# Attention by hand-ordered matmuls: inverse roots by log and exp, other buffers for the compression weights, memory heads further apart, half of the convolution taps held back

## The chip, the cores and the metric

The kernel runs on one core of a Trainium2 chip. The metric is the device time of one execution in microseconds (us); the median of three runs is compared. The engines are called as the profile calls them: PE (matrix products; PEld its weight loads), DVE (vector), ACT (scalar and activation), POOL (general), SP (whose queue issues the DMAs).

## The reference

Two transformer blocks are applied to 256 tokens of width 1024, in float32. Block one mixes stick-breaking attention and gated linear attention (GLA), then a squared-ReLU MLP. Block two is a hybrid layer:

```
q_nsa, kv_nsa, g_nsa, conv_in, q_mem, g_merge = split(rms_norm(x) @ w_in)
kc = rms_norm(compress(k_c)); vc = compress(v_c)     # compress: gelu(blocks @ w1) @ w2
o_nsa = g[0]*attend(q, kc, vc) + g[1]*attend(q, ks, vs) + g[2]*attend(q, kw, vw)   # 8 heads, g = sigmoid(g_nsa)
u = silu(layer_norm(depthwise_conv31(a * sigmoid(ag)) + conv_b))   # 512 channels
o_m = softmax(qm @ km.T) @ vm                        # 4 memory heads of 128, 256 memory tokens
merged = gm[0]*(o_nsa @ w_nsa_out) + gm[1]*(u @ w_conv_out) + gm[2]*(o_m @ w_mem_out)   # gm = sigmoid(g_merge)
h = x + merged @ w_out;  out = h + (silu(hn @ w_gate) * (hn @ w_up)) @ w_down
```

## The kernel before, in words

**The stream of weights.** Every float32 operand of a large product is split into a high and a low part. A chunk of weights (128 x 1024, 512 KB) is brought by SP into one of four buffers `raw`, ACT casts it to `hi` (L519, three buffers), DVE subtracts to get `lo` (L523, three buffers), and PE adds hi times hi, hi times low and lo times high (L325, L327, L329: eight matmuls each for a column tile with eight row blocks). So each chunk needs SP, ACT, DVE and PE in this order, and a `hi` buffer is free when PE has finished with it. Buffers are taken in turn: a chunk that is late holds up the one three places behind it.

**Who sets the order.** A scheduler lists the instructions by priority (`tc.high_priority` raises it, `tc.issue_after` forbids an instruction before another one) and fixes for each engine one order. On the chip each engine works through its order strictly, so an instruction that waits holds up all behind it. In block two's attention the order on PE is written by hand (`manual_schedule`): `fill(gates, n)` puts n halves of a merge gate's column tile (`gm`, one chunk each) between the steps of the attention, as work that needs nothing of the attention. DVE, ACT and SP are ordered by the scheduler there too.

**Block two's attention, by its functions.** `compress` multiplies the keys and values by the compression weights `wc1` (L1213) and ends with a gelu that is written with a sigmoid (`cmp_t`, `cmp_h`) and a norm of the compressed keys (`cmp_k`, `cmp_kn`, L1256 to L1260). `nsa_operands` sums squares by head (L1276), takes an inverse root by integer shift and three Newton steps (`rsqrt`, twelve small DVE instructions, L385 to L391, into `hn_y`) and transposes it (L1291). `nsa` runs eight score blocks `first(n)`, transposes (`turned`, L1393), products (`values`, L1407) and the compressed branch (L1329). `mem_attention` is a generator with three parts for each of four memory heads: scores (L1461) and softmax; transposes of the probabilities P (L1476); product with the values (L1482), whose result is split into `om`. `conv_taps` adds 31 shifted products for each of four channel groups on DVE (L1494, L1496), and `conv_norm` makes the layer norm from them: a mean over channels by a matmul (L1511), a subtraction, squares, token sums (L400), an inverse root of two columns (twelve DVE instructions), its transpose back (L407), a product, a sigmoid and the split `uc`. Behind the attention stand three products with the branches' output weights: `wmo` (operand `om`), `wno` (operand `on`), `wco` (operand `uc`).

**Block one.** In GLA, `gla_scores` takes a gate's decay by a cumulative sum, six pairs of scaled operands `lev` (L779 to L783, two of the products on POOL or DVE), and masks sums `lvm` (L813, L816).

Of the kernel before, what the change touches and what calls it, by code (L numbers as in the profile page):

```python
# [183 lines left out]
class Kern:  # L184
# [65 lines left out]
    def load_constants(self):  # L250
# [123 lines left out]
    def rsqrt(self, v, n, y=None):  # L374

        nc = self.nc
        if n > 16:
            ti, hv, t = self.small("rw_i", [128, n], I32, bufs=1), *(self.small(s, [128, n], bufs=1) for s in ("rw_h", "rw_t"))
        else:
            ti = self.gsmall("rs_i", [128, 16], I32)[:, :n]  # L380
            hv = self.gsmall("rs_h", [128, 16])[:, :n]
            t = self.gsmall("rs_t", [128, 16])[:, :n]
# [41 lines left out]
    def split(self, h, l, src, gain=None):  # L424
# [4 lines left out]
        if gain is None:  # L429
            nc.scalar.copy(h, src)  # L430
            nc.vector.tensor_tensor(l, src, h.bitcast(F32), op=OP.subtract)
        else:
            nc.scalar.activation(h, src, AF.Copy, scale=gain)
            nc.vector.scalar_tensor_tensor(l, src, gain, h.bitcast(F32), op0=OP.mult, op1=OP.subtract)

# [122 lines left out]
def block_one(K, B, after):  # L558
# [4 lines left out]
    st = K.stream("w1a")  # L563
    for q in range(4):
# [12 lines left out]
    for k in range(8):  # L577
        xk = xin[k // 4][:, (k % 4) * 256:(k % 4) * 256 + 256]
        K.split(X.h(k), X.l(k), xk, par["norm_mix"][:, k:k + 1])
    for q in range(4):  # L580
        sqs.add(xin[q // 2][:, (q % 2) * 512:(q % 2) * 512 + 512])
    rc, rr = None, None
# [22 lines left out]
    def norm():  # L605
        nonlocal rc, rr
# [105 lines left out]
def gla_scores(K, glow, wgu, gq, gk):  # L712
# [22 lines left out]
    K.tap("c", c)  # L735

# [36 lines left out]
    def level(w):  # L773
# [8 lines left out]
        nc.gpsimd.tensor_tensor(gv[:, :, 1], ev[:, :, 1], qv[:, :, 1], op=OP.mult)  # L782
# [14 lines left out]
    for pr in range(3):  # L797
# [17 lines left out]
        if pr:  # L815
            nc.gpsimd.tensor_tensor(m, m, sums, op=OP.add)  # L816
# [9 lines left out]
def gla_values(K, SS, gv, og):  # L826
# [4 lines left out]
    for h in range(4):  # L831
# [9 lines left out]
        nc.gpsimd.tensor_tensor(s[:, :256], s[:, :256], s[:, 256:], op=OP.add)  # L841
# [189 lines left out]
def block_two(K, B, KM, vm, out):  # L1031
# [54 lines left out]
    with tc.manual_schedule(engines={mybir.EngineType.PE}):  # L1086
# [7 lines left out]
        nc.vector.tensor_tensor(gn, K.gemm_n(K.narrow("wgn", B.gain), B.x), rr, op=OP.mult)  # L1094
# [9 lines left out]
        s4 = nc.scalar.activation(N.gate, pg, AF.Sigmoid)  # L1104
# [6 lines left out]
        with tc.issue_after(s3.ins), tc.issue_after(s4.ins), tc.issue_after(N.sig.ins):  # L1111
# [3 lines left out]
    conv_taps(K, u, cv)  # L1115
# [70 lines left out]
def compress(K, kc2, N):  # L1186
# [381 lines left out]
```

## Time and profile before

| what | value |
|---|---|
| median of three runs | 945.62 us (944.42 to 948.03) |
| the profiled execution's own time | 948.07 us |
| its span | 946.3 us |
| PE busy | 907.4 us (96%) |
| DVE busy | 675.7 us (71%) |
| ACT busy | 495.6 us (52%) |
| POOL busy | 69.7 us (7%) |
| mean granted TensorE clock | 0.982 |

The span runs from the first to the last instruction; the time of the run holds 1.8 us more. The profiled execution took 2.45 us longer than the median. PE has work for nearly the whole span, so what can be taken away is mainly its idle time and the time in which its clock is granted at half. The clock has two levels, 1.2 and 2.4 GHz; a granted clock of 0.50 in a row is the lower one.

### The profile page before, as it was taken

Reading aid. Unit: us, or ns where it says so; the run is one execution under the profiler, and the core shown is the slowest. Engines: PE = TensorE matmul, PEld = TensorE weight load, DVE = VectorE, ACT = ScalarE, POOL = GpSimd, SP = SyncE. Lnnn points to the kernel's source line nnn. Section 1 sums busy time; section 2 is a strip of 40 time slices with the busy share of each in tenths; the row PEclk is TensorE's granted clock in tenths of the full one; section 3 lists DMA queues with packets and bytes.
Section 4 is the critical chain, followed back from the end, with each engine's and each line's share of the span. In section 5 each row is a group of like instructions: output and inputs, shape, how many; then the busy total and the mean of one; then the engine's idle time right before and its main releaser. Section 6 shows DMA issues by size and latency. Waiting matters only on the chain.

```text
span 946.3 us, 17011 instructions
## 1 busy us (share of the span) xinstructions
PE 907.4 (96%) x6816; PEld 834.7 (88%) x6816; DVE 675.7 (71%) x1167; ACT 495.6 (52%) x745; POOL 69.7 (7%) x94
## 2 busy tenths in 40 slices
PE   8988999999999999999999886988899999999998
PEld 6986789999999999888999786977799988888887
DVE  6698758857776665556568958897488878888653
ACT  5555665644555554444443245666854655555432
POOL 1022012200010000011200000000003200000000
PEclk9999999999999999999999979899999999999999
DMA  7644325665756566566655743222346556666672
GB/s 268 200 128 128 102 70 155 217 201 178 223 179 183 184 189 181 157 184 192 185 174 167 266 124 112 68 89 90 112 117 191 184 176 181 187 191 182 192 208 65
DMA packets 44287, 155.64 MB, mean 164 GB/s; under 512 B 5040, under 2 KB 6576, under 8 KB 44208
## 3 DMA queue, kind: packets, MB, share of 16 engines
q1 hardware_dynamic: 43776, 153.48, 52.4%
q8 instruction: 53, 0.87, 0.4%
q10 hardware_dynamic: 432, 1.08, 0.4%
q14 instruction: 26, 0.21, 0.1%
HBM read 153.49 MB, written 1.05 MB: 163 GB/s over the span
## 4 chain that ended last, share of the span: by engine, by line
PE 85%; DVE 6%; ACT 4%; DMA 2%; issue 2%; POOL 1%; SPq 0%; DVEq 0%; ACTq 0%; POOLq 0%
PE pj L296 17%; PE pj L325 15%; PE pj L327 14%; PE pj L329 14%; PE pj L297 9%; PE pj L368 5%; DVE lo L523 2%; ACT hi L519 2%; PE pj L310 1%; PE pj L311 1%; PE pj L309 1%; DVE cv L1496 1%; DMA raw<-in_w2a_dram 1%; POOL lev L782 1%; PE pt L1276 1%
## 5 line engine op out<-in xcount | busy, mean ns | idle before, releaser
L519 ACT CAST hi<-raw 128x1024 fp32r<-128x1024 f32 x276 | 288.3, 1047 | 302.3 <-PE pj L327 125.7
L523 DVE TENSOR_TENSOR lo<-raw,hi 128x1024 fp32r<-128x1024 f32 x276 | 343.0, 1244 | 116.7 <-ACT hi L519 110.7
L296 PE MATMUL pj<-hid,hi 128*128 128x512 f32 x378 | 134.3, 400 | 0.0
L296 PE MATMUL pj<-xf,hi 128*128 128x512 f32 x320 | 113.2, 399 | 0.0
L297 PE MATMUL pj<-hid,lo 128*128 128x256 f32 x378 | 106.2, 281 | 0.0
L297 PE MATMUL pj<-xf,lo 128*128 128x256 f32 x320 | 89.8, 281 | 0.0
L296 PEld LDWEIGHTS pj<-hid,hi 128*128 128x128 f32 x378 | 71.0, 188 | 17.5
L296 PEld LDWEIGHTS pj<-xf,hi 128*128 128x128 f32 x320 | 60.1, 188 | 14.8
L297 PEld LDWEIGHTS pj<-hid,lo 128*128 128x128 f32 x378 | 71.4, 189 | 0.0
L297 PEld LDWEIGHTS pj<-xf,lo 128*128 128x128 f32 x320 | 60.4, 189 | 0.0
L325 PE MATMUL pj<-xm,hi 128*128 128x256 f32 x336 | 55.1, 310 | 0.0
L325 PEld LDWEIGHTS pj<-xm,hi 128*128 128x128 f32 x336 | 48.5, 209 | 4.2 <-issue 2.7
L1496 DVE SCALAR_TENSOR_TENSOR cv<-u,par,cv 128x256 f32<-128x256 f32 x120 | 51.5, 477 | 0.0
L472 POOL TENSOR_TENSOR acc<-acc,ffr 128x256 f32<-128x256 f32 (+1 forms) x25 | 27.3, 1099 | 311.4 <-ACT ffr L465 288.9
L327 PE MATMUL pj<-xm,hi 128*128 128x256 f32 x336 | 49.7, 293 | 0.0
L329 PE MATMUL pj<-xm,lo 128*128 128x256 f32 x336 | 47.9, 286 | 0.0
L327 PEld LDWEIGHTS pj<-xm,hi 128*128 128x128 f32 x336 | 46.2, 204 | 0.0
L327 PE MATMUL pj<-xn,hi 128*128 128x256 f32 x304 | 44.2, 285 | 0.0
L329 PEld LDWEIGHTS pj<-xm,lo 128*128 128x128 f32 x336 | 44.2, 195 | 0.0
L329 PE MATMUL pj<-xn,lo 128*128 128x256 f32 x304 | 43.9, 284 | 0.0
L325 PE MATMUL pj<-xn,hi 128*128 128x256 f32 x304 | 43.5, 285 | 0.0
L329 PEld LDWEIGHTS pj<-xn,lo 128*128 128x128 f32 x304 | 39.5, 192 | 0.5 <-issue 0.4
(464 smaller groups left out, 1653.3 us busy)
## 6 DMA issues: line engine op xcount, KB each, us to landing
raw<-in_wf_dram SPq DMA_DIRECT2D x64, 512.0 KB, 3.7
raw<-in_wgu_dram SPq DMA_DIRECT2D x44, 512.0 KB, 3.7
raw<-in_w1g_dram SPq DMA_DIRECT2D x24, 512.0 KB, 3.7
raw<-in_w2g_dram SPq DMA_DIRECT2D x24, 512.0 KB, 3.7
raw<-in_wdn_dram SPq DMA_DIRECT2D x22, 512.0 KB, 3.7
raw<-in_w2a_dram SPq DMA_DIRECT2D x20, 512.0 KB, 3.7
raw<-in_w1a_dram SPq DMA_DIRECT2D x16, 512.0 KB, 4.7
raw<-in_wo_dram SPq DMA_DIRECT2D x16, 512.0 KB, 3.7
```

The costliest lines, as they stand in the source:

```text
L296: mm(ps, lhsT=st.hi(w), rhs=x.both(k), start=k == 0, stop=False, skip_group_check=True)
L297: mm(ps[:, :T], lhsT=st.lo(w), rhs=x.h(k), start=False, stop=k == kt - 1, skip_group_check=True)
L309: mm(ps[:, j], lhsT=st.hi(w), rhs=x.h(k), start=k + j == 0, stop=False, skip_group_check=True)
L310: mm(ps[:, j], lhsT=st.hi(w), rhs=x.l(k), start=False, stop=False, skip_group_check=True)
L325: mm(ps[:, j], lhsT=st.hi(o + k), rhs=x.h(k), start=k == 0, stop=False)
L327: mm(ps[:, j], lhsT=st.hi(o + k), rhs=x.l(k), start=False, stop=False)
L329: mm(ps[:, j], lhsT=st.lo(o + k), rhs=x.h(k), start=False, stop=k == kt - 1)
L368: mm(pss[t], lhsT=xx(k)[:, t * 128:t * 128 + 128], rhs=ww(o + k), start=k == 0 and xx == x.h and ww == st.hi, stop=k == kt - 1 and ww == s ...
L472: self.engine.tensor_tensor(a, a, s, op=OP.add)
L519: nc.scalar.copy(hi, raw)
L523: eng.tensor_tensor(lo[:, o:o + n], raw[:, o:o + n], hi[:, o:o + n].bitcast(F32), op=OP.subtract)
L1496: nc.vector.scalar_tensor_tensor(o, u[:, c, k:k + 256], w[:, c, k:k + 1], o, op0=OP.mult, op1=OP.add)
```

## The change

It has five groups of edits.

- **Start.** A fourth warm-up matmul; the first two chunks of `w1a` are brought, cast and subtracted in halves (`st.halved`); the splits of the input get priorities and the squares stand behind the last of them.
- **Block one.** The decay of GLA is computed in a function of its own (`gla_decay`) and called in the norm's lead; twelve instructions go from POOL to DVE: six `lev` products, two `lvm` sums and four sums `ffr`.
- **Compression weights.** They are brought as 16 DMAs of 128 x 512 into the four buffers `P1` of the attention's probabilities instead of 8 of 128 x 1024 into `raw`.
- **Sigmoid and inverse root.** Both sigmoids (gates and gelu) become max, Exp, plus one, reciprocal; the inverse roots of `hn_y` and of `cmp_k` become Ln, Exp and three DVE instructions (one Newton step).
- **Memory heads and taps.** The parts of a memory head stand further apart among the `fill(gates, 1)`; the taps of channel groups 2 and 3 may be issued only behind the softmax denominators of score blocks 4 and 7 (`N.marks`).

```diff
@@ start
-            for _ in range(3):
-                nc.tensor.matmul(p, lhsT=z[:, :128], rhs=z, start=True, stop=True)
+            for n in (512, 512, 512, 256):
+                nc.tensor.matmul(p[:, :n], lhsT=z[:, :128], rhs=z[:, :n], start=True, stop=True)
...
+    st.halved = (0, 1)
...
+        with tc.high_priority(offset=800000 - 50000 * k):
+            last = K.split(X.h(k), X.l(k), xk, par["norm_mix"][:, k:k + 1])
+    with tc.issue_after(last.ins):
+        for q in range(4):
+            sqs.add(xin[q // 2][:, (q % 2) * 512:(q % 2) * 512 + 512])
@@ block one
             nc.vector.tensor_tensor(glow, ps, rr, op=OP.mult)
+            decay = gla_decay(K, glow, wgu)
...
-        nc.gpsimd.tensor_tensor(gv[:, :, 1], ev[:, :, 1], qv[:, :, 1], op=OP.mult)
+        nc.vector.tensor_tensor(gv[:, :, 1], ev[:, :, 1], qv[:, :, 1], op=OP.mult)
...
-            nc.gpsimd.tensor_tensor(m, m, sums, op=OP.add)
+            nc.vector.tensor_tensor(m, m, sums, op=OP.add)
...
-        nc.gpsimd.tensor_tensor(s[:, :256], s[:, :256], s[:, 256:], op=OP.add)
+        nc.vector.tensor_tensor(s[:, :256], s[:, :256], s[:, 256:], op=OP.add)
@@ compress
-            with K.tc.high_priority(offset=100000):
-                raw = K.wp.tile([128, 1024], F32, tag="raw", name=K.nm("wc1"), bufs=4)
-                nc.sync.dma_start(raw, K.a["wc1"][kv * 4 + ch])
             for j in range(4 * ch, 4 * ch + 4):
-                w = raw[:, (j % 4) * 256:(j % 4) * 256 + 256]
+                if j % 2 == 0:
+                    raw = K.small("P1", [128, 2, 256], bufs=4)
+                    with K.tc.high_priority(offset=100000):
+                        nc.sync.dma_start(raw, K.a["wc1"][kv * 4 + ch][:, (j % 4) * 256:(j % 4) * 256 + 512])
...
-    N.sig = nc.scalar.activation(t, t, AF.Sigmoid, scale=2 * (2 / np.pi) ** 0.5)
+    sigmoid(K, t, t, 2 * (2 / np.pi) ** 0.5)
...
-    y = K.rsqrt(k2, 16)
+    y = rsqrt_exp(K, k2, *(K.small(n, [128, 16], bufs=1) for n in ("cmp_y", "cmp_w")))
+def sigmoid(K, out, x, scale=1.0):
+    K.nc.vector.tensor_scalar(out, x, -87.0 / scale, None, op0=OP.max)
+    K.nc.scalar.activation(out, out, AF.Exp, scale=-scale)
+    K.nc.vector.tensor_scalar(out, out, 1.0, None, op0=OP.add)
+    K.nc.vector.reciprocal(out, out)
+def rsqrt_exp(K, v, y, t):
+    nc.scalar.activation(t, v, AF.Ln)
+    nc.scalar.activation(y, t, AF.Exp, scale=-0.5)
+    nc.vector.tensor_tensor(t, y, y, op=OP.mult)
+    nc.vector.scalar_tensor_tensor(t, t, -0.5, v, op0=OP.mult, op1=OP.mult)
+    nc.vector.scalar_tensor_tensor(y, t, 1.5, y, op0=OP.add, op1=OP.mult)
@@ nsa
+        N.marks[n] = nc.vector.tensor_tensor(den, den, gate[:, :, 3 * h + 1:3 * h + 3], op=OP.mult)
...
         values(i)
-        if m:
-            finish(m)
         fill(gates, 1)
+        if i:
+            next(late[-1 - (i == 3)])
         if i < 3:
-            m = mem(i)
-            next(m)
+            late.append(mem(i))
+            next(late[-1])
+        fill(gates, 1)
+        if i:
+            finish(late[-2])
+        if i < 2:
             fill(gates, 1)
@@ block_two, conv_taps
-    conv_taps(K, u, cv)
+    conv_taps(K, u, cv, {2: N.marks[4], 3: N.marks[7]})
...
+        with K.tc.issue_after(behind[c].ins) if c in behind else nullcontext():
```

The edits shift the lines: in the changed kernel L325, L327, L329 are L324, L326, L328; L523 is L522; L1461, L1476, L1482 are L1497, L1512, L1518; L1496 is L1534; L1511, L400, L407 are L1549, L396, L403.

**PE, memory head 0.** Ahead of the change these rows stand on PE (con is the identity that a transpose multiplies by; pj is a column tile's sum, hi and lo are named by their chunk):

```order
L1461 MATMUL pt_6668<-km_2500,qm_5252 128x256 x2
L325 MATMUL pj_6637<-xm_4405,hi_6683 128x256 x2
...
L329 MATMUL pj_6637<-xm_4408,lo_6684 128x256 x2
L1393 MATMUL pt_6712<-con,P_950_6499 128x128
...
L1476 MATMUL pt_6724<-con,P_982_6675 128x128 x4
```

And with the change:

```order
L1497 MATMUL pt_6680<-km_2507,qm_5259 128x256 x2
L324 MATMUL pj_6649<-xm_4412,hi_6695 128x256 x2
...
L324 MATMUL pj_6724<-xm_4412,hi_6727 128x256 x2
...
L324 MATMUL pj_6724<-xm_4412,hi_6796 128x256 x2
...
L324 MATMUL pj_6837<-xm_4412,hi_6840 128x256 x2
...
L324 MATMUL pj_6837<-xm_4412,hi_6909 128x256 x2
...
L1512 MATMUL pt_6938<-con,P_986_6687 128x128 x4
```

Between the scores of the head and the transposes of its probabilities stood one chunk of gates; now five stand there, with attention steps among them.

**PE, the convolution's norm.** Before, the token sums and the transposed inverse root stood in these rows:

```order
L400 MATMUL pt_7584<-con,ffr_7574 128x1 x2
L329 MATMUL pj_7382<-xm_4405,lo_7421 128x256 x2
...
L325 MATMUL pj_7649<-om_5235,hi_7652 128x256 x2
...
L329 MATMUL pj_7649<-om_5236,lo_7653 128x256 x2
L325 MATMUL pj_7713<-om_5235,hi_7716 128x256
L407 MATMUL pt_7605<-con,rs_y_7592 128x128 x2
```

Now they stand here, behind most of the tiles of `wmo` and `wno`:

```order
L326 MATMUL pj_7855<-on_5240,hi_7858 128x256 x2
L326 MATMUL pj_7855<-on_5241,hi_7858 128x256 x2
L328 MATMUL pj_7855<-on_5240,lo_7859 128x256 x2
L328 MATMUL pj_7855<-on_5241,lo_7859 128x256
L396 MATMUL pt_7596<-con,ffr_7586 128x1 x2
L328 MATMUL pj_7855<-on_5241,lo_7859 128x256
L403 MATMUL pt_7617<-con,rs_y_7604 128x128 x2
L324 MATMUL pj_7693<-om_5242,hi_7696 128x256 x2
```

Half a gate tile and more than a whole `om` tile (33 matmuls in all) stood between the two; now one matmul stands there.

**DVE, the end of the attention.** From the last split of `on`, DVE had these rows before (L1513 is the subtraction of the convolution's mean):

```order
L431 TENSOR_TENSOR on_5234<-pt_7327,on_5234 128x256
L431 TENSOR_TENSOR om_5236<-pt_7339,om_5236 128x256
L1070 TENSOR_TENSOR gm_5242<-pj_7296,rr_5359 128x512
L523 TENSOR_TENSOR lo_7653<-raw_7650,hi_7652 128x1024
L1513 TENSOR_TENSOR cv_5243<-cv_5243,pt_7575 128x1024
```

And with the change:

```order
L427 TENSOR_TENSOR on_5241<-pt_7363,on_5241 128x256
L1534 SCALAR_TENSOR_TENSOR cv_5250<-u_5257,par,cv_5250 128x256 x5
L522 TENSOR_TENSOR lo_7697<-raw_7694,hi_7696 128x1024
L1534 SCALAR_TENSOR_TENSOR cv_5250<-u_5257,par,cv_5250 128x256 x4
L522 TENSOR_TENSOR lo_7729<-raw_7726,hi_7728 128x1024
L1082 TENSOR_TENSOR gm_5249<-pj_7375,rr_5366 128x512
L427 TENSOR_TENSOR om_5243<-pt_7444,om_5243 128x256
L1534 SCALAR_TENSOR_TENSOR cv_5250<-u_5257,par,cv_5250 128x256 x3
L427 TENSOR_TENSOR om_5243<-pt_7456,om_5243 128x256
L1534 SCALAR_TENSOR_TENSOR cv_5250<-u_5257,par,cv_5250 128x256 x5
```

All taps stood ahead of this place before; now groups of one to five stand between the rows that PE waits for, 33 of them behind `N.marks[7]`, and the fold of the convolution's sums follows the last.

## Rows read from the trace of the kernel before

**Rows 1.** Page of the profile: busy us, share of the span, instructions of PE.

```profile
...
PE 907.4 (96%) x6816; PEld 834.7 (88%) x6816; DVE 675.7 (71%) x1167; ACT 495.6 (52%) x745; POOL 69.7 (7%) x94
...
```

**Rows 2.** Waits of PE: us in total, times, longest us.

```profile
...
PE pt L1476 <- DVE P L1471: 7.3, 3, 2.7
PE pt L1329 <- DVE cmp_kn L1260: 5.1, 1, 5.1
PE pj L368 <- ACT hi L519: 3.7, 1, 3.7
PE pt L1482 <- DVE on L431: 3.4, 3, 1.6
PE pt L1291 <- DVE hn_y L391: 2.4, 1, 2.4
PE pj L310 <- DVE xn L434: 2.1, 2, 1.3
...
```

**Rows 3.** Windows: stretch in us, busy us by engine, granted clock, DMA share.

```profile
...
55.00:85.00 30.00, 24.82 (x532) 20.54 (x531) 28.23 (x36) 13.67 (x17) 13.75 (x8) 1.00 0.33 103
618.00:642.00 24.00, 20.61 (x150) 18.77 (x149) 22.80 (x69) 14.73 (x38) 0.00 (x0) 0.93 0.26 83
642.00:696.00 54.00, 46.69 (x340) 43.00 (x339) 31.08 (x76) 38.05 (x69) 0.00 (x0) 0.94 0.32 101
...
```

**Rows 4.** Windows, same columns: stretches of half clock.

```profile
...
546.50:549.90 3.40, 2.99 (x14) 2.99 (x15) 3.40 (x5) 2.91 (x4) 0.00 (x0) 0.50 0.62 167
...
621.60:625.00 3.40, 3.40 (x16) 3.21 (x15) 2.92 (x14) 1.65 (x5) 0.00 (x0) 0.50 0.30 119
...
```

**Rows 5.** Timeline of PE: start, us, instruction, idle time before it.

```profile
...
616.80 1.12 PE L329 MATMUL pj<-xm,lo 128*128 128x256 f32 x8
617.77 0.82 PE L1393 MATMUL pt<-con,P 128*128 128x128 f32 x6
...
622.71 1.91 PE L325 MATMUL pj<-xm,hi 128*128 128x256 f32 x8
...
```

**Rows 6.** Timeline of all engines at the window value projection w2v.

```profile
...
539.75 2.85 DVE L1496 SCALAR_TENSOR_TENSOR cv<-u,par,cv 128x256 f32<-128x256 f32 x7
...
544.10 1.04 ACT L519 CAST hi<-raw 128x1024 fp32r<-128x1024 f32 x1 [3.83 <-DMA raw<-in_w2v_dram]
...
546.91 0.58 PE L368 MATMUL pj<-hi,xm 128*128 128x256 f32 x1 [1.33 <-DVE glow L1094]
...
```

**Rows 7.** Timeline of POOL in block one's attention.

```profile
...
60.39 1.79 POOL L782 TENSOR_TENSOR lev<-lev,gq 128x512 f32<-128x512 f32 x1 [31.62 <-ACT lev L781]
...
```

**Rows 8.** Timeline of DVE in the same stretch.

```profile
...
60.35 0.69 DVE L783 TENSOR_TENSOR lev<-lev,gk 128x512 f32<-128x512 f32 x1
...
67.89 2.30 DVE L523 TENSOR_TENSOR lo<-raw,hi 128x1024 fp32r<-128x1024 f32 x1
...
```

**Rows 9.** Timeline of DVE across both inverse roots.

```profile
...
561.69 0.23 DVE L1282 TENSOR_SCALAR hn_v<-pt,b_v 128x16 f32<-128x16 f32 x1 [5.98 <-PE pt L1276]
...
573.29 0.19 DVE L391 SCALAR_TENSOR_TENSOR hn_y<-rw_t,hn_y 128x32 f32<-128x32 f32 x1
...
590.80 0.19 DVE L1260 TENSOR_TENSOR cmp_kn<-cmp_k,con 128x32 f32<-128x32 f32 x1
...
```

**Rows 10.** Groups of DVE instructions from 615 to 696 us: busy, mean ns.

```profile
...
L523 DVE TENSOR_TENSOR lo<-raw,hi 128x1024 fp32r<-128x1024 f32 x15 | 18.3, 1222 | 8.7 <-ACT hi L519 8.5
...
L1070 DVE TENSOR_TENSOR gm<-pj,rr 128x512 f32<-128x512 f32 x7 | 4.8, 690 | 6.1 <-PE pj L329 6.1
...
```

**Rows 11.** Timeline of PE around the convolution's norm.

```profile
...
695.05 0.61 PE L400 MATMUL pt<-con,ffr 128*128 128x1 f32 x4
...
699.68 0.43 PE L407 MATMUL pt<-con,rs_y 128*128 128x128 f32 x2
...
```

**Rows 12.** Timeline of DVE in the same stretch.

```profile
...
690.38 1.22 DVE L1513 TENSOR_TENSOR cv<-cv,pt 128x1024 f32<-128x1024 f32 x1
...
707.91 0.75 DVE L431 TENSOR_TENSOR uc<-cv,uc 128x256 fp32r<-128x256 f32 x2
...
```

More of the change, by code (lines that the diff above doesn't have):

```diff
@@ L1 @@
-from contextlib import contextmanager
+from contextlib import contextmanager, nullcontext
 import numpy as np
@@ L376, in rsqrt @@
         nc = self.nc
[L377 to L382, printed above, removed]
+        ti = self.gsmall("rs_i", [128, 16], I32)[:, :n]
+        hv = self.gsmall("rs_h", [128, 16])[:, :n]
+        t = self.gsmall("rs_t", [128, 16])[:, :n]
         if y is None:
@@ L578, in block_one @@
         xk = xin[k // 4][:, (k % 4) * 256:(k % 4) * 256 + 256]
[L579 to L582, printed above, removed]
+        with tc.high_priority(offset=800000 - 50000 * k):
[3 more added lines that the diff above has]
+            sqs.add(xin[q // 2][:, (q % 2) * 512:(q % 2) * 512 + 512])
+    rc, rr, decay = None, None, None
     glow = K.gsmall("glow", [128, T], bufs=1)
@@ L605, in norm @@
     def norm():
-        nonlocal rc, rr
+        nonlocal rc, rr, decay
         ps = K.gemm_n(gl, xin)
@@ L709, in lo, with gla_decay @@
         return self.st.lo(t + self.o)
-def gla_scores(K, glow, wgu, gq, gk):
+def gla_decay(K, glow, wgu):
     nc = K.nc
@@ L735, in gla_scores @@
     K.tap("c", c)
+    return c
+def gla_scores(K, c, gq, gk):
+    nc = K.nc
+    mm = nc.tensor.matmul
     def v(x, w):
@@ L1093, in block_two @@
         next(cmp)
[L1094 removed]
+        pn = K.gemm_n(K.narrow("wgn", B.gain), B.x)
+        with tc.high_priority(offset=50000):
+            nc.vector.tensor_tensor(gn, pn, rr, op=OP.mult)
         next(cmp)
@@ L1103, in block_two @@
         N.gate = K.small("gate", [128, 2, 24], bufs=1)
-        s4 = nc.scalar.activation(N.gate, pg, AF.Sigmoid)
+        with tc.issue_after(s3.ins):
+            nc.scalar.preload_act_table_set("natural_log_exp_and_others")
+            sigmoid(K, N.gate, pg)
         gates = K.steps_b(K.stream("w2g"), 8, 24, B.X, evg)
@@ L1216, in compress @@
                 yield
+    part = K.small("P1", [128, 2, 256], bufs=4)
     nc.scalar.copy(part, pa)
@@ L1278, in nsa_operands @@
         at += n * m
-    v, y = (K.small(n, [128, 32], bufs=1) for n in ("hn_v", "hn_y"))
+    v, y, w = (K.small(n, [128, 32], bufs=1) for n in ("hn_v", "hn_y", "hn_w"))
     y3 = y.rearrange("p (t n) -> p t n", t=2)
@@ L1354, in nsa @@
     cz = con["causal0"]
-    S = {}
+    S, N.marks = {}, {}
     def first(n):
@@ L1419, in nsa @@
     fill(gates, 1)
-    m = None
+    late = []
     for i in range(4):
         turned(2 * i)
-        if m:
-            next(m)
-        if i == 3:
-            fill(gates, 1)
-            m2 = mem(i)
-            next(m2)
-        else:
-            first(2 * i + 2)
+        if i < 3:
+            first(2 * i + 2)
+        else:
+            late.append(mem(3))
+            next(late[-1])
         fill(gates, 1)
@@ L1438, in nsa @@
         values(i)
-        if m:
-            finish(m)
         fill(gates, 1)
+        if i:
+            next(late[-1 - (i == 3)])
         if i < 3:
-            m = mem(i)
-            next(m)
+            late.append(mem(i))
+            next(late[-1])
+        fill(gates, 1)
+        if i:
+            finish(late[-2])
+        if i < 2:
             fill(gates, 1)
-    next(m2)
+    next(late[-1])
     fill(gates, 1)
-    finish(m2)
-    return S["last"]
+    finish(late[-1])
+    return N.last
 def mem_attention(K, N, KM, vm, OM):
@@ L1485, in mem_attention, with conv_taps @@
     return head
-def conv_taps(K, u, cv):
+def conv_taps(K, u, cv, behind):
     nc, par, con = K.nc, K.par, K.con
```

53 lines of the change are left out of this document (29 added, 24 removed).

## The prediction

> **What bounds the kernel now.** I read the page first. PE is busy 907.4 us of the span [rows 1] of 946.3, so 38.9 us are idle in all, and no change can give back more than that plus what a half clock takes. The list of waits of PE says where it is idle: the largest groups lie in block two's attention [rows 2]. The transposes of the memory heads (L1476) wait 7.3 us for the probabilities, the products of the heads (L1482) 3.4, the compressed branch (L1329) 5.1, the value projection w2v (L368) 3.7 for its first chunk, the transposed inverse root (L1291) 2.4. Block one's attention shows no long wait but many short ones: in 55 to 85 us PE is busy 24.82 of 30 [rows 3]. The splits of the input cost 2.1 at the start [rows 2].
>
> The windows show a second cost. Behind each of the three waits of L1476, which are 2.4 us long on average and 2.7 at most [rows 2], the clock is granted at 0.50 (1.2 GHz) for 3.4 us; the first such stretch stands in [rows 4], and the eight first matmuls of a column tile take 1.91 us there against 1.12 for eight at 2.4 GHz [rows 5]. Eight at full clock move PE on by 0.97 us, from 616.80 to 617.77 [rows 5], that is 0.12 a matmul and 2.9 a chunk of gates (24 of them). So such a stretch, when PE is full in it, costs half of it, 1.7 us. A stretch like it follows the stall at w2v; PE is busy 2.99 of it, which makes 1.5 [rows 4]. In 642 to 696 us the mean clock is 0.94 [rows 3]: half clock for 0.12 of 54 us, two such stretches, behind the waits of heads 1 and 2.
>
> **The change part by part.** A minus is time saved.
>
> *Start.* Three short idle times, 2.1 of them on `xn` [rows 2], stand against halved chunks and splits with priority. The work before the first product stays; only its order changes. Bounds 0.3 (one of the waits shortened) to 1.2; I take **-0.6**.
>
> *Block one.* The idle 5.2 us [rows 3] are shared by waits for `lev`, `kq` and `sbk`. A POOL product takes 1.79 us where the like DVE product takes 0.69, and a `lo` beside POOL's products takes 2.30 us [rows 7, 8] where its mean elsewhere is 1.22 [rows 10]. Moving twelve instructions puts on DVE eight of 0.69 and four of 256 columns, about 0.42 as for the taps, 7.2 us; but seven DVE instructions between 61 and 83 us lay beside POOL and lost some 6.6 in all (the longest is the row shown), so DVE gets most of it back, and the chain by POOL's product shortens by 1.1 each time. DVE was busy 28.23 of the 30 us [rows 3], so it stays the neighbour that decides. `gla_decay` now runs some ten us earlier, beside column tiles that wait for nothing in it. Bounds -1 and -5.5; I take **-4**, as both causes of the waits are touched and a few short ones will stay.
>
> The rule against this edit: the Trainium skill, "Perfetto Trace Analysis", section "Optimizing Scalar/DVE Operations", says that a saturated DVE should rather give work away, and that moving it between GpSimd and DVE might not help since the two share a read port. The lengthened `lo` fits the shared port [rows 8]. By the rule alone the move is worth nothing and only the earlier decay counts, about -2.5, and the sum below is 1.5 higher; by the rows it is -4.
>
> *Compression weights.* Before, the eight chunks `wc1` went through the buffers `raw`, so `w2v` was asked for late: ACT idles 3.83 us for its DMA, and PE 3.7 [rows 2] and then 1.33 us [rows 6], 5.0 in all, and the half clock adds 1.5. Now `wc1` has the buffers `P1`, four of 16 pieces are there long before, and `raw` is free. SP's queue runs strictly in order: twelve pieces wait for a step of `compress`, and `w2v`, `w2g` stand between them. Each step frees two pieces some 3 us ahead of their use, and as many bytes move as before. I count 0.3 left: **-6.2**. Bounds: 0 (w2v late again) and -6.5.
>
> *Sigmoid and inverse roots.* The chain from `hn_v` to `hn_y` takes 11.8 us for twelve instructions of 0.2 [rows 9], because it stands between `lo`s that wait for casts. Five instructions shorten it, but two of them are on ACT, behind a cast that waits for a free `hi`, and `cmp_h` (which PE needs ahead of L1326, the old L1291) stands behind a `lo` and a `gm` that needs the end of the column tile. The cast (1.05), the `lo` and the `gm` (0.69) start when the tile's last weights leave, so PE waits 2 to 2.5 us there instead of 2.4 [rows 2]: **0**, bounds 2 either way. For `cmp_kn` [rows 9] the same count leaves a wait of 2.9 of 5.1 [rows 2]: **-2.2**, bounds 0 and -4.
>
> *Memory heads.* The softmax took at most 2.7 us longer than the one chunk of gates that covered it [rows 2]. Five chunks are 11.5 us more cover, and the step from transposes to products, late by 1.6 at most, gets a chunk of its own, so L1476's 7.3 and L1482's 3.4 go [rows 2], and three half-clock stretches (1.7 each) with them: **-15.8**. Bounds: -10.7 (the stretches stay) and -15.8.
>
> *Held taps.* 62 taps of 0.41 us (2.85 us for seven [rows 6]), 25.4 us, stand behind the marks. In 642 to 696 us DVE is busy 31.08 of 54 [rows 3], but the change takes some 11 us of idle and half clock out of that stretch. Counted over the changed order from mark 4 to the fold of the taps, with the durations of the groups [rows 10]: DVE 61.4 us of work, PE 62.3. DVE is as full as PE, so each `lo`, `gm` and `om` that stands behind a group of taps can come late, and the chunks behind wait for `hi`. Against a heavy price: in 618 to 642 us DVE is busy 22.80 of 24 [rows 3], and PE waits there only for the memory head. Bounds: nothing, and the 33 taps behind mark 7 in full, 13.5. I take **+5**, nearer to the full row than to the whole 13.5.
>
> *The convolution's norm.* From the token sums to the transposed root PE had 4.63 us [rows 11], filled with 33 matmuls. DVE had a `gm`, a `lo` and twelve small instructions in that time, and it has the same now, but one matmul covers it: +4.4. The `lo` behind the subtraction of 1.22 us [rows 12] makes the tile before wait: +1.2. From the transposed root to the first two parts `uc` are 9.0 us [rows 11, 12], and PE has 72 matmuls of 0.12 [rows 5] there in the changed order, 8.6: +0.7 with the lateness of DVE. Idle times of 2.4 us brought half-clock stretches [rows 2, 4]: +1.7. In all **+8**; bounds 2 (other instructions of PE arrive late, so the chain is ahead) and 10.
>
> **The sum.** -0.6 - 4 - 6.2 - 2.2 - 15.8 = -28.8; +5 + 8 = +13; together -15.8. The profiled execution would take 948.07 - 15.8 = 932.3 us, its span 930.5. It was 2.45 above the median, so the median goes from 945.62 to 929.8: I say **930**.
>
> **The rivals.**
>
> *The end is covered.* If DVE keeps up and the norm's chain is done before PE comes, the +13 shrink to 3: 920. For it: DVE's 95% in rows 3 without other waits. Against: one matmul between sums and root.
>
> *DVE decides.* If the 33 last taps come to stand on the path (13.5) and the starts of `hi` slip with them, the losses are 20 to 24: 937 to 941. For it: 61.4 against 62.3.
>
> *The change does not do what it says at w2v.* SP's queue stands at a piece for `P1` while `w2v` is behind it; then the 6.2 are not saved: 936. For it: two pieces stand ahead of each `w2v` chunk. Against: four were brought early.
>
> *Slower.* All 62 held taps (25.4) lie on the path, as DVE has no time left beside `lo`, and the norm's 8 with its bound 10: -28.8 + 25.4 + 10 = +6.6, 952. It decides from the point where more than 21 of the 25.4 us come on the path. Against it: 0.9 us of slack plus the waits that remain.
>
> **How the numbers follow.** Main case 0.48 (its own range 925 to 936); covered end 0.18 (917 to 925); w2v 0.08; DVE decides 0.20 (936 to 945); slower 0.06. The range leaves out the better half of the covered end and the worst of the last two: 920 to 941, where the bounds of the end (2 to 10) and of the taps (0 to 13.5) lie too. About 0.5% (4.7 us) is what a measurement can tell from no change. Faster holds the first three cases and half of DVE decides, 0.84; the same 0.10, the rest of that case and the mild part of the last; slower 0.06.
>
> **What would show it.** In the profile of the changed kernel L1512 and L1518 should be out of PE's waits and the clock whole from 615 to 690; L367 should wait under 1 us for `hi`; L1257 or L1326 should show 2 to 2.5, L1364 about 3; L403 should wait about 4 us for `rs_y`, a half-clock stretch behind it; DVE should be over 90% busy for the 60 us before. POOL should be nearly empty in 55 to 85, with `lo` at 1.22. The prediction is wrong if L403 shows no wait, if `lo` is late through the heads, or if SP waits at `P1`.

## The result and the profile after

The changed kernel took 931.1 us (median of four runs, 926.79 to 932.48) against 945.27 for the kernel before (four runs as well; 945.62 was the median of three of them): a ratio of 0.9835, with a 95% interval of 0.9814 to 0.9857. The forecast was 930, with a range of 920 to 941. The profiled execution took 931.74 us against 948.07, so 16.3 went; the sum had been 15.8.

The page of the profile after (span, then busy us of the engines):

```profile
span 929.9 us, 17029 instructions
...
PE 903.5 (97%) x6818; PEld 831.3 (89%) x6818; DVE 680.2 (73%) x1169; ACT 491.6 (53%) x747; POOL 52.7 (6%) x82
...
```

PE's idle time (span less busy) fell from 38.9 us to 26.4. PE's own busy time fell by 3.9, and its mean granted clock rose from 0.982 to 0.987, so fewer matmuls ran at half clock. The list of waits of PE (us in total, times, longest), to be read against [rows 2]:

```profile
...
PE pt L403 <- DVE rs_y L387: 5.5, 3, 5.0
PE pt L822 <- issue: 2.9, 2, 2.5
PE pt L1257 <- DVE hn_y L1294: 2.6, 1, 2.6
PE pt L1364 <- DVE cmp_kn L1276: 2.0, 1, 2.0
...
PE pj L328 <- DVE lo L522: 0.8, 1, 0.8
...
PE pj L324 <- ACT hi L520: 0.7, 1, 0.7
PE pj L326 <- DVE uc L427: 0.6, 1, 0.6
...
PE pj L324 <- ACT om L426: 0.5, 1, 0.5
PE pt L1518 <- DVE om L427: 0.3, 1, 0.3
...
```

The transposes of the memory heads, L1476's 7.3 us before, are gone from the list (L1512 is their line now), the products (L1518) wait 0.3, and `hi` for the projection w2v is no longer waited for. L1257 has taken over the wait of L1291 with 2.6 us for 2.4. Two long waits are new: L403, the transposed root of the convolution's norm, and 2.9 us at L822 in block one that the profile puts down to nothing it knows ("issue").

The windows that answer to [rows 3] (busy us of PE, PEld, DVE, ACT, POOL, then the granted clock):

```profile
...
55.00:85.00 30.00, 26.99 (x522) 23.28 (x520) 23.67 (x36) 12.21 (x13) 0.00 (x0) 1.00 0.44 131
618.00:642.00 24.00, 24.00 (x191) 21.97 (x188) 23.39 (x73) 16.08 (x40) 0.00 (x0) 1.00 0.42 120
642.00:680.00 38.00, 36.48 (x283) 33.97 (x282) 36.38 (x75) 25.44 (x43) 0.00 (x0) 1.00 0.39 119
680.00:692.00 12.00, 6.09 (x44) 5.39 (x44) 9.68 (x22) 3.15 (x3) 2.08 (x1) 0.95 0.42 132
...
```

Block one's PE is busy 26.99 of 30 us, with no work on POOL. From 618 to 642 us PE is full at full clock while DVE is busy for 23.39 of 24. From 642 to 680 DVE is at 96%. Behind that PE is busy for only 6.09 of 12 us. The timeline of PE there, answering to [rows 11]:

```profile
...
686.41 0.36 PE L328 MATMUL pj<-on,lo 128*128 128x256 f32 x1
691.81 0.69 PE L403 MATMUL pt<-con,rs_y 128*128 128x128 f32 x2 [5.03 <-DVE rs_y L387]
692.15 1.20 PE L324 MATMUL pj<-om,hi 128*128 128x256 f32 x4
...
```

One matmul covers what 33 covered before, and PE waits 5.03 us. What DVE does in that time, answering to [rows 12]:

```profile
...
686.59 0.16 DVE L1556 TENSOR_SCALAR rms_v<-pt 128x2 f32<-128x2 f32 x1 [0.83 <-PE pt L396]
...
687.42 1.22 DVE L522 TENSOR_TENSOR lo<-raw,hi 128x1024 fp32r<-128x1024 f32 x1
688.56 1.23 DVE L381 TENSOR_SCALAR rs_i<-rms_v 128x2 int32<-128x2 int32 x1
689.70 0.16 DVE L383 TENSOR_SCALAR rs_h<-rms_v 128x2 f32<-128x2 f32 x1
...
691.59 0.16 DVE L387 SCALAR_TENSOR_TENSOR rs_y<-rs_t,rs_y 128x2 f32<-128x2 f32 x1
...
```

A `gm`, the `lo`, then the twelve small instructions of the root, as forecast, with one surprise: the first, `rs_i` (128 x 2), takes 1.23 us where the next takes 0.16. POOL adds two gate tiles at that time, and `rs_i` ends at 689.79, 0.03 us behind that addition:

```profile
...
687.68 2.08 POOL L1152 TENSOR_TENSOR gm<-gm,gm 128x512 f32<-128x512 f32 x1 [211.87 <-DVE gm L1150]
...
```

Two half-clock stretches of interest are left, one behind L403 and one behind L1257 (columns as above):

```profile
...
690.70:697.50 6.80, 5.69 (x27) 5.70 (x28) 4.91 (x15) 3.15 (x6) 0.00 (x0) 0.50 0.08 33
564.40:567.80 3.40, 3.40 (x39) 2.89 (x37) 2.06 (x8) 0.00 (x0) 0.00 (x0) 0.50 0.42 143
...
```

PE is busy 5.69 of the first 6.80 us, so it costs some 2.8; the second costs 1.7. SP's queue at the projection (issue time, us, transfer):

```profile
...
518.10 0.33 SPq L515 DMA_DIRECT2D raw<-in_w2v_dram  x1
...
521.61 0.33 SPq L515 DMA_DIRECT2D raw<-in_w2v_dram  x1
...
```

And before:

```profile
...
537.48 0.80 SPq L516 DMA_DIRECT2D raw<-in_w2v_dram  x2
...
```

The first chunk of `w2v` is issued at 518.10 us; before, it was issued at 537.48.

The places at which PE starts some products split the 16.4 us of the span. (The first product with `og`, the output of block one's attention; the end of the waits for `cmp_h` or `hn_y` and for `cmp_kn`; the first product with `mrg`, the merged branches.)

| up to | before | after | gained in the stretch | forecast |
|---|---|---|---|---|
| first `og` | 219.0 | 216.2 | 2.8 | 4.6 (start 0.6, block one 4) |
| start of the wait at L1291 / L1257 | 571.1 | 561.4 | 6.9 | 6.2 |
| end of that wait | 573.5 | 564.1 | -0.2 | 0 |
| end of the wait for `cmp_kn` | 591.0 | 579.2 | 2.4 | 2.2 |
| first `mrg` | 731.5 | 715.6 | 4.0 | 2.8 (15.8 less 5 and 8) |
| end | 946.3 | 929.9 | 0.5 | 0 |

The sum fits, and most stretches do. What a stretch holds can still be wrong in both directions, so the experiments take the edits apart.

### The profile page after: what moved, and what is told of

Read it like the earlier page. It is cut to its first block, busy times and chain, and to the rows that moved or that the text cites. A ratio compares the mean times of both kernels' runs of the same rounds, so it can differ in the third digit from the quotient of the medians.

```text
span 929.9 us, 17029 instructions
## 1 busy us (share of the span) xinstructions
PE 903.5 (97%) x6818; PEld 831.3 (89%) x6818; DVE 680.2 (73%) x1169; ACT 491.6 (53%) x747; POOL 52.7 (6%) x82
## 4 chain that ended last, share of the span: by engine, by line
PE 91%; DVE 5%; ACT 1%; issue 1%; DMA 0%; SPq 0%; DVEq 0%; ACTq 0%
PE pj L295 17%; PE pj L324 16%; PE pj L326 16%; PE pj L328 15%; PE pj L296 9%; PE pj L367 5%; DVE lo L522 2%; PE pj L309 1%; PE pj L310 1%; PE pj L308 1%; ACT hi L520 1%; PE pt L1311 1%; PE pt L913 1%; PE pt L1442 1%; PE pt L403 1%
## 5 line engine op out<-in xcount | busy, mean ns | idle before, releaser
L520 ACT CAST hi<-raw 128x1024 fp32r<-128x1024 f32 (+1 forms) x278 | 288.6, 1041 | 306.9 <-PE pj L326 139.2
L522 DVE TENSOR_TENSOR lo<-raw,hi 128x1024 fp32r<-128x1024 f32 (+1 forms) x278 | 339.8, 1224 | 105.2 <-ACT hi L520 97.2
L1534 DVE SCALAR_TENSOR_TENSOR cv<-u,par,cv 128x256 f32<-128x256 f32 x120 | 53.8, 476 | 1.2
L324 PE MATMUL pj<-xm,hi 128*128 128x256 f32 x336 | 52.1, 299 | 0.0
L324 PEld LDWEIGHTS pj<-xm,hi 128*128 128x128 f32 x336 | 45.7, 198 | 4.9 <-ACT hi L520 2.5
L326 PE MATMUL pj<-xm,hi 128*128 128x256 f32 x336 | 48.5, 288 | 0.0
L328 PE MATMUL pj<-xm,lo 128*128 128x256 f32 x336 | 47.2, 283 | 0.0
L328 PE MATMUL pj<-xn,lo 128*128 128x256 f32 x304 | 44.8, 286 | 0.0
L326 PEld LDWEIGHTS pj<-xm,hi 128*128 128x128 f32 x336 | 44.7, 198 | 0.0
L326 PE MATMUL pj<-xn,hi 128*128 128x256 f32 x304 | 44.0, 285 | 0.0
L324 PE MATMUL pj<-xn,hi 128*128 128x256 f32 x304 | 43.8, 285 | 0.0
L328 PEld LDWEIGHTS pj<-xm,lo 128*128 128x128 f32 x336 | 43.5, 193 | 0.0
L328 PEld LDWEIGHTS pj<-xn,lo 128*128 128x128 f32 x304 | 39.7, 192 | 0.5 <-issue 0.4
```

The costliest lines, as they stand in the source:

```text
L324: mm(ps[:, j], lhsT=st.hi(o + k), rhs=x.h(k), start=k == 0, stop=False)
L326: mm(ps[:, j], lhsT=st.hi(o + k), rhs=x.l(k), start=False, stop=False)
L328: mm(ps[:, j], lhsT=st.lo(o + k), rhs=x.h(k), start=False, stop=k == kt - 1)
L520: nc.scalar.copy(hi[:, o:o + n], raw[:, o:o + n])
L522: nc.vector.tensor_tensor(lo[:, o:o + n], raw[:, o:o + n], hi[:, o:o + n].bitcast(F32), op=OP.subtract)
L1534: nc.vector.scalar_tensor_tensor(o, u[:, c, k:k + 256], w[:, c, k:k + 1], o, op0=OP.mult, op1=OP.add)
```

## The experiments

Twelve kernels ran, in three groups of four; the kernel before ran beside each group and had medians of 944.6, 944.97 and 945.53 us. The group of e4 to e7 ran on another chip than the other two. All but e8_heads_only start from the changed kernel.

| run | median us | ratio to before, 95% interval |
|---|---|---|
| the change (first, and again) | 931.1, 932.63 | 0.9835 [0.9814, 0.9857], 0.9863 [0.9842, 0.9883] |
| e1_taps_free | 922.96 | 0.9771 [0.9739, 0.9804] |
| e1b_taps_24 | 921.48 | 0.9758 [0.9729, 0.9787] |
| e3_heads_old | 929.46 | 0.9846 [0.9811, 0.9881] |
| e8_heads_only (on the kernel before) | 931.94 | 0.9861 [0.9828, 0.9894] |
| e4_wc_raw | 935.47 | 0.9898 [0.9862, 0.9934] |
| e5_pool | 933.86 | 0.9886 [0.9859, 0.9913] |
| e6_old_roots | 932.82 | 0.9866 [0.9842, 0.9890] |
| e7_decay_late | 925.41 | 0.9788 [0.9764, 0.9813] |
| r9_both_undone | 917.51 | 0.9705 [0.9679, 0.9732] |
| r10_gelu_first | 918.6 | 0.9711 [0.9691, 0.9731] |
| r11_old_heads_free_taps | 935.86 | 0.9899 [0.9880, 0.9918] |

**Taps not held (e1_taps_free).**

```diff
-    conv_taps(K, u, cv, {2: N.marks[4], 3: N.marks[7]})
+    conv_taps(K, u, cv, {})
```

> The change with the taps not held (nothing behind N.marks). Theory: the 8.5 us at the convolution's norm (5.0 wait of L403, 2.8 of half clock, 0.6 at uc) and some 2 us of late hi and lo behind the taps come from the held taps alone; with the taps free the norm stands on PE 35 matmuls of cover between token sums and root and 148 between root and uc, so the time falls to 920 to 923, L403 waits under 1 us and no half clock is seen near 690. Rival: the taps were held because DVE is full in 595 to 645 us; then the memory heads' waits or the lo's come back there and eat it up: 928 to 934, with PE idle 3 us or more in 590 to 650.

Its waits of PE:

```profile
...
PE pt L1428 <- DVE P L1418: 2.7, 1, 2.7
...
PE pt L1518 <- DVE om L427: 0.8, 1, 0.8
...
PE pj L324 <- ACT om L426: 0.5, 1, 0.5
PE pt L403 <- DVE rs_y L387: 0.4, 2, 0.2
...
```

8.1 us faster, L403 waits no longer (its 0.4 is two waits of the kind that every run has), and no half clock stands near 690. The theory holds. The rival's effect is there, but small: one wait of 2.7 us for P (L1428) at 588 us, with a half-clock stretch behind it, which the held taps had avoided. The late `hi` and `lo` ahead of the norm are gone from the list; the waits for `om` are not (0.8 and 0.5), so they do not come from holding.

**Taps held earlier (e1b_taps_24).**

```diff
-    conv_taps(K, u, cv, {2: N.marks[4], 3: N.marks[7]})
+    conv_taps(K, u, cv, {2: N.marks[2], 3: N.marks[4]})
```

> The change with groups 2 and 3 of the taps held behind N.marks[2] and N.marks[4] in place of 4 and 7. Theory (the norm's lateness is what the holding costs): the norm stands on PE as it does with free taps, so 920 to 924, the same as with free taps within 2 us. Rival (DVE is full before, holding helps the early part): faster than free taps by 2 us or more.

```profile
...
PE pt L1428 <- DVE P L1418: 0.5, 1, 0.5
...
PE pt L403 <- DVE rs_y L387: 0.4, 2, 0.2
...
```

L1428 is back at 0.5 and L403 at 0.4. The gain of 1.5 us over free taps is inside both intervals: which of the two is faster stays open. The profiles of this kernel and of the change agree within 0.1 us up to the end of the wait for `cmp_kn` (579.2 us), and the first `uc` then starts at 693.6 us here and at 703.2 in the change: 9.6 us, which is also the difference of the medians. Holding itself is not what costs; holding until mark 7 is.

**Memory heads at the old distance (e3_heads_old).** The loop over heads in `nsa` is that of the kernel before; the marks stay.

```diff
...
         values(i)
+        if m:
+            finish(m)
         fill(gates, 1)
-        if i:
-            next(late[-1 - (i == 3)])
         if i < 3:
-            late.append(mem(i))
-            next(late[-1])
-        fill(gates, 1)
-        if i:
-            finish(late[-2])
-        if i < 2:
+            m = mem(i)
+            next(m)
             fill(gates, 1)
...
```

> The change with the memory heads at their old distance. Theory: the spacing is worth the 11 us of waits of L1476 and L1482 and three half-clock stretches, 15.8 in all, so 944 to 948 with L1512 waiting about 7 us in three waits; a part may come back, since the norm has 49 matmuls of cover between sums and root in this order: not under 938. Rival: with shorter sigmoids and other DVE work most of the wait was gone anyway: 931 to 935.

```profile
...
PE pt L1511 <- DVE P L1506: 5.8, 3, 2.0
PE pt L1517 <- DVE on L427: 3.3, 3, 1.3
...
PE pt L403 <- DVE rs_y L387: 0.4, 2, 0.2
...
```

The waits are back as expected, 9.1 us in six, with half-clock stretches behind two of them, and still the kernel is not slower than the change. My expectation of 944 to 948 was wrong, and the bound "not under 938" with it: L403 waits 0.4 here. In the trace of this order 47 matmuls stand between token sums and root and 149 between root and `uc`, so PE waits neither for the root nor for `uc`. So distance and holding had to be separated in both directions.

**Old distance and free taps (r11_old_heads_free_taps).** The edit is that of e3_heads_old with that of e1_taps_free.

> The change with the memory heads at the old distance and the taps not held. Theory: distance and holding do not add up. The distance is worth its waits and half clock (some 14 us) where the taps are free, and next to nothing where they are held, since the norm is late only with both: 935 to 938. Rival (they add up: old distance costs nothing, holding costs 8): 920 to 923.

```profile
...
PE pt L1511 <- DVE P L1506: 5.8, 3, 2.2
PE pt L1517 <- DVE on L427: 3.8, 3, 1.8
...
```

935.86. With free taps the new distance is worth 935.86 - 922.96 = 12.9 us; with taps held to mark 7 it is worth 929.46 - 931.1 = -1.6 (-3.2 by the change's second median), nothing within the intervals. The two edits share one place: each alone leaves the norm covered, and both together put it behind the last tiles.

**The new distance alone (e8_heads_only).** The kernel before with the new loop over the heads and nothing else.

> The kernel before with the new distance of the memory heads alone; taps as before. Theory: the 15.8 us of the heads are gained whole, as taps and norm are early: 945.3 - 15.8 = 929 to 931, no half clock behind 595 us. Rival (the gain needs the held taps, since DVE is full): 934 to 942 with PE waits in 600 to 650 us.

```profile
...
PE pt L407 <- DVE rs_y L391: 0.4, 2, 0.2
...
```

931.94, which is 12.7 faster than the kernel before beside it (944.6), somewhat less than the 15.8 of the sum, and L407 waits for no root. The distance alone gives 932, everything but the distance (e3_heads_old) gives 929, and both together 931: most of the one's gain is lost in the other.

**POOL's instructions back (e5_pool) and the decay late (e7_decay_late).**

```diff
-        nc.vector.tensor_tensor(gv[:, :, 1], ev[:, :, 1], qv[:, :, 1], op=OP.mult)
+        nc.gpsimd.tensor_tensor(gv[:, :, 1], ev[:, :, 1], qv[:, :, 1], op=OP.mult)
...
-            nc.vector.tensor_tensor(m, m, sums, op=OP.add)
+            nc.gpsimd.tensor_tensor(m, m, sums, op=OP.add)
...
-        nc.vector.tensor_tensor(s[:, :256], s[:, :256], s[:, 256:], op=OP.add)
+        nc.gpsimd.tensor_tensor(s[:, :256], s[:, :256], s[:, 256:], op=OP.add)
```

> The change with the twelve instructions of block one's attention on POOL again (lev, lvm, ffr), the decay still early. Theory: POOL's products lengthen lo and lev on DVE (up to 2.3 us for a lo of 1.22) and the chain over POOL's product is 1.1 us longer each time, so PE's idle time in 45 to 85 us grows from about 4 to 6 or more: 933 to 934. Rival (the shared port makes the move worth nothing): 930.5 to 931.5.

```diff
-            decay = gla_decay(K, glow, wgu)
...
-        SS = gla_scores(K, decay, gq, gk)
+        SS = gla_scores(K, gla_decay(K, glow, wgu), gq, gk)
```

> The change with the decay of GLA computed where it was before, at the head of gla_scores; its twelve instructions stay on DVE. Theory: scores wait for the decay again: some 1 to 2 us more idle in 45 to 85 us, 932 to 933. Rival (the decay's place decides nothing, the move from POOL does all): 930.5 to 931.5.

With POOL, PE waits for its `lev` (L804 and L822), and the window from 55 to 85 us is less full than the change's 26.99:

```profile
...
PE pt L822 <- DVE lev L795: 2.3, 2, 1.4
PE pt L804 <- POOL lev L794: 2.3, 1, 2.3
...
PE pt L822 <- POOL lev L794: 0.9, 1, 0.9
...
```

```profile
...
55.00:85.00 30.00, 25.44 (x533) 22.75 (x532) 24.53 (x30) 12.01 (x13) 10.60 (x6) 0.98 0.33 102
...
```

With DVE and a late decay it is the fullest of all, DVE too, with no wait of "issue":

```profile
...
55.00:85.00 30.00, 28.96 (x549) 23.58 (x549) 29.39 (x47) 19.59 (x27) 0.00 (x0) 1.00 0.43 141
...
```

The first product with `og` starts at these times (us), in all profiles:

| decay | `lev`, `lvm`, `ffr` on | first `og` |
|---|---|---|
| late | POOL (two profiles, with the old start) | 219.0 |
| early | POOL (e5_pool, with a half-clock stretch at 52.6) | 222.0 |
| early | DVE (four profiles without a half-clock stretch up to there; the change's first run: 216.2) | 215.6 to 216.2 |
| early | DVE (four with one; the change's second run: 217.8) | 217.2 to 217.9 |
| late | DVE (three profiles) | 213.8 to 214.4 |

So the move from POOL is worth some 4 us up to there: 4.1 to 4.9 with the early decay, like compared with like for the half clock, and 3.6 to 4.2 with the late one, when 1.0 is taken off for the start. The early decay costs 1.2 to 2.4, and 2.8 to 4.1 where a half-clock stretch follows. The time of e5_pool came as expected (933.86, 1.2 to 2.8 above the change's two medians), which is less than the 4 us; its profile is of the slowest of its four runs. The sign of my expectation for the decay was wrong.

The median of e7_decay_late is 5.7 us below the change's first and 7.2 below its second. Of the 6.2 us between the two profiled executions (931.74 and 925.54), 2.4 lie ahead of `og`, 1.9 between `og` and `mrg`, where e7_decay_late had a half-clock stretch of 6.8 us at the head sums for the change's 10.2, and 2.0 in a stretch of the last large products. That stretch took 123.3 us in the profiles of e4 to e7 and 125.3 in all others, so the medians of e4 to e7 may lie up to 2.0 too low beside the change's. Whether they do stays open: the kernel before, which has the same stretch, was not faster beside them (944.97).

What the early decay costs is the wait at L822. It stands in all eight profiles with an early decay on DVE, begins at 74.6 to 75.2 us and lasts 1.9 to 2.5; in four of them, the change's second run among them, a half-clock stretch follows it, which the change's first run did not have:

```profile
...
PE pt L822 <- issue: 2.8, 2, 1.9
...
```

```profile
...
78.50:81.90 3.40, 3.40 (x10) 2.63 (x9) 3.32 (x6) 0.57 (x1) 0.00 (x0) 0.50 0.23 35
...
```

PE waits there in the middle of equal matmuls of 32 columns whose operands were used just before. In the same 3 us of the change's first run the DMA queue for instructions moves one packet (0.02 MB):

```profile
...
q8 instruction: 1, 0.02, 2.8%
...
```

In all eight the pause ends 1.2 to 1.5 us behind the end of such a packet (16 KB), and the shorter pause of 0.4 to 0.8 us at 68 to 69 us stands behind another one in the same way (1.3 to 1.6 us). Not every packet brings a pause: those at 61 and 78 us do not, and with the late decay PE pauses behind none of them, but for 0.5 us in r10_gelu_first. So it is likely that PE waits for its own instructions. The trace does not say which engine's instructions a packet holds, and that the early decay brings the pause by letting two bursts of small matmuls follow each other closely is argued, not shown.

**Compression weights in `raw` (e4_wc_raw).**

```diff
-                if j % 2 == 0:
-                    raw = K.small("P1", [128, 2, 256], bufs=4)
-                    with K.tc.high_priority(offset=100000):
-                        nc.sync.dma_start(raw, K.a["wc1"][kv * 4 + ch][:, (j % 4) * 256:(j % 4) * 256 + 512])
+            with K.tc.high_priority(offset=100000):
+                raw = K.wp.tile([128, 1024], F32, tag="raw", name=K.nm("wc1"), bufs=4)
+                nc.sync.dma_start(raw, K.a["wc1"][kv * 4 + ch])
...
```

> The change with the compression weights in the stream's buffers raw again, 8 DMAs of 128x1024. Theory: w2v is late again, about 5 us of PE idle at L367 and a half-clock stretch behind it: 937 to 938 against the change's 931. Rival (the heads of the stream are late from the small buffers as well, so nothing is gained): 930 to 933.

```profile
...
PE pj L367 <- DVE glow L1108: 1.6, 1, 1.6
...
PE pj L367 <- ACT hi L520: 0.8, 1, 0.8
...
```

935.47: 2.8 to 4.4 us slower than the change's two medians, with 2.4 of waits at L367 and a half-clock stretch behind them, not 5. From the first `og` to the wait at L1257 its profile needs 348.7 us against 345.3 and 345.6 in the change's two, 3.1 to 3.5 more. If its runs were all as fast in the last products as its profile, the medians lie up to 2.0 further apart. The queue's order up to `w2v` is that of before, so I put the rest of the stall down to the transfer itself. Median time from issue to landing of the two `w2v` chunks, in the kernel before, in e4_wc_raw and in e8_heads_only, which has the old buffers as well (KB each, median us):

```profile
...
raw<-in_w2v_dram SPq DMA_DIRECT2D x2, 512.0 KB, 7.0
...
```

```profile
...
raw<-in_w2v_dram SPq DMA_DIRECT2D x2, 512.0 KB, 4.2
...
```

```profile
...
raw<-in_w2v_dram SPq DMA_DIRECT2D x2, 512.0 KB, 5.0
...
```

The profiled execution of before had the longest landing of the three. The stall of 5.0 us that the forecast removed was 1.8 to 2.6 us longer than in the two others (3.2 in e8_heads_only, 2.4 in e4_wc_raw).

**Old sigmoids and roots (e6_old_roots).** `K.rsqrt` and `AF.Sigmoid` as before, at both places, with their scratch buffers, and `nsa` issued behind both sigmoids again.

> The change with the sigmoids and the inverse roots as before (Sigmoid on ACT, integer start and three Newton steps on DVE). Theory: the wait ahead of L1326 is set by the lo and gm of the tile and not by the root, so it stays at 2 to 2.6 us; cmp_kn is 2.5 to 3 us later: 933 to 934. Rival (ACT's table changes between Exp and Sigmoid come into the softmaxes): 936 or more.

```profile
...
PE pt L1366 <- DVE cmp_kn L1278: 3.1, 1, 3.1
PE pt L1328 <- DVE hn_y L390: 3.1, 1, 3.1
...
```

932.82, the same as the change within the intervals (its group is the one whose medians may be up to 2.0 too low). L1328 (the old L1291) waits 3.1 instead of 2.6, more than the 2 to 2.6 that I named, and L1366 (the old L1329) 3.1 instead of 2.0, 1.6 in all. The new forms save that in waits; in time it is not clear of noise. Of the fall of `cmp_kn`'s wait from 5.1 to 2.0 they make 1.1; the other 2.0 come with the other edits.

**The change again (r12_change_again).** 

> The change as it is, for a comparison on the same chip as the three beside it: 929 to 932 by every theory. The wait of L822 of 2 to 3 us that no semaphore explains should stand at the same place, if it belongs to the order of the instructions and not to one execution.

932.63, with the waits of the first profile at the same places, L822 among them.

**Both costs undone (r9_both_undone).** The edits of e7_decay_late and e1b_taps_24 together.

> The change with the taps behind N.marks[2] and N.marks[4] and the decay of GLA late, as before. If the two gains seen alone are of different places, as the theory has it (8.5 us at the convolution's norm and some 1.5 of late casts; 2.4 us of a wait of L822 that no semaphore explains), they add up: 917 to 919, with no wait at L403 and none at L822. Rival (the late decay's gain of 5.7 in the medians was mostly a faster stretch of that run's last products): 919 to 922.

```profile
span 918.4 us, 17036 instructions
...
```

917.51, 15.1 us below the change on the same chip and 28 below the kernel before. The two gains add up: `og` starts 4.0 us earlier than in the change's second run, and from there to the first `uc` it takes 8.9 us less. L403 waits 0.4 and L822 not at all. This version beats both kernels.

**The gelu ahead of the tile's `lo` (r10_gelu_first).**

```diff
-    sigmoid(K, t, t, 2 * (2 / np.pi) ** 0.5)
-    nc.vector.tensor_tensor(h, h, t, op=OP.mult)
+    with K.tc.high_priority(offset=150000):
+        sigmoid(K, t, t, 2 * (2 / np.pi) ** 0.5)
+        nc.vector.tensor_tensor(h, h, t, op=OP.mult)
...
-    rsqrt_exp(K, v, y, w)
+    with K.tc.high_priority(offset=150000):
+        rsqrt_exp(K, v, y, w)
```

> As r9_both_undone, and the gelu's sigmoid, its product cmp_h and the inverse root hn_y get a priority that puts them on DVE ahead of the lo and gm of the column tile. Theory: the wait of L1257 (2.6 us) is that lo and gm, not the root itself; it falls under 0.6, and the half-clock stretch of 3.4 us behind it goes: 3 to 4 us faster than r9. Rival (the sigmoid chain itself is as late): the wait stays at 2 or more and the time is that of r9 within 1 us.

```profile
...
PE pt L1365 <- DVE cmp_kn L1276: 2.8, 1, 2.8
PE pt L1429 <- ACT P L1412: 2.4, 1, 2.4
...
```

L1257 falls from 2.3 (r9_both_undone) to 0.4 us, and the half-clock stretch behind it goes, so the wait was the `lo` and the `gm`, as the forecast had it. But the time, 918.6, is the same, where I expected 3 to 4 us: L1365 rises from 2.0 to 2.8, and a new wait of 2.4 us stands at L1429, with a half-clock stretch behind it. The gain was spent 14 and 29 us later.

## Why the prediction was right, and where its steps were not

The signs that the prediction named came: the clock whole from 615 to 690 us, L403 at 5.0 (about 4 named) with half clock behind it, DVE at 96% ahead of it, POOL empty in 55 to 85. L1364 waits 2.0 instead of 3.

*Start:* right in sign, undersized. The idle times ahead of the first full products fell from 2.9 to 2.3 us, 0.6 as taken, but the first of those products (L325, now L324) starts at 15.8 us instead of 16.9, so the start gave 1.0.

*Block one:* right in sign, wrong in one cause. Forecast 4, seen 1.8 in the change's first profile (2.8 less the start's 1.0) and next to nothing in its second. The prediction gave the move from POOL 1.5 and the early decay 2.5; the move is worth some 4, and the early decay costs. The step that failed is that the early decay runs "beside column tiles that wait for nothing in it". PE does not wait for its DVE and ACT work there, but the pause at L822 comes with it, and 1.2 to 4.1 us go back.

The Trainium skill, "Perfetto Trace Analysis", "Optimizing Scalar/DVE Operations", says that moving work between GpSimd and DVE might not help because of the shared read port. Here it helped by some 4 us at `og`, and the measurement decides: the `lev` of POOL was slower by itself (1.79 against 0.69 us), and a DVE `lo` beside POOL's work took 2.30 us [rows 7, 8]. The port it speaks of fits `rs_i` with its 1.23 us beside POOL's addition; no run separates the port from other causes.

*Compression weights:* right in mechanism and in the stretch (6.9 for 6.2), but undoing it costs 3.1 to 3.5 in the stretch and 2.8 to 4.4 in the medians, perhaps 2.0 more. The term was read from one execution with a landing of 7.0 us, whose stall was 1.8 to 2.6 us longer than in the two others; how much of the 6.9 belongs to that execution stays open.

*Sigmoid and roots:* 0 at L1257, for the reason given, as r10_gelu_first shows. For `cmp_kn` 2.4 in the stretch for 2.2, but by e6_old_roots only 1.1 of the wait is the new forms' doing: the size came out in part by luck.

*Memory heads:* mechanism right, size 13 for 15.8, where the taps are early. Part of the rest is a cost that the sum did not have: PE now waits 0.8 and 0.5 us for `om`, also with free taps (e1_taps_free, e8_heads_only).

*Held taps:* 5 taken, under 1 seen: the waits that go with free taps ahead of the norm are two for `hi`, 0.66 and 0.13 us. The row with DVE at 95% [rows 3] was the better guide than the upper bound. *Norm:* 8 taken, seen 5.0 at L403, 0.75 for the `lo` behind the subtraction, 0.6 at `uc` and 2.8 of half clock, 9.2. In the 5.0 are 1.1 us of `rs_i` beside POOL, which the forecast did not have.

The weak point is the form of the sum. It gave the heads -15.8 and the end +13 as two independent terms. The runs show one term: held taps without the new distance, or the new distance without held taps, leave the norm covered. The total came out since both were in the change, and since two errors of some 3 us cancel: the heads gave 13 and not 15.8, the end took 9.6 (e1b_taps_24; 8.1 by e1_taps_free) and not 13. That is luck.

## What to carry to other kernels

When work is held back to make room for a stall, look at what waits for the last of it: 62 taps of 0.41 us cost under 1 us in late operands of PE and some 9 us where PE had no cover left for the chain behind them. Undo edits in pairs and not one by one, since two edits can be worth 13 us and nothing by turns. Read the price of a stall on a transfer, or of a wait with half clock behind it, from more than one execution.

## What the runs showed of the hardware that was not expected

- PE paused for about 2 us amid equal small matmuls, at the same place in eight profiles, with no releaser in the trace; each time it went on 1.2 to 1.5 us behind the end of a packet of 16 KB of the DMA queue for instructions.
- A DVE instruction of 128 x 2 took 1.23 us instead of 0.17 while POOL added two tiles of 128 x 512 (2.08 us), and ended 0.03 us behind that addition.
- At the head sums (L1311) the granted clock was 0.50 for 10.2 us in r9_both_undone and for 6.8 in r10_gelu_first, with the same order of PE up to there; half of the 3.4 us, 1.7, is what that alone can move an execution by.
- One stretch of 736 matmuls took 123.3 us in the four profiles of e4 to e7, on one chip, and 125.3 in the others; the cause was not tried.
